# When the first layer's last block pair loads, adds and queues its P4 chunks

## The chip, the cores and the metric

The kernel runs on one core of a Trainium2 chip. The metric is the device time of one execution in microseconds (us), lower is better. PE is TensorE, DVE is VectorE, ACT is ScalarE, POOL is GpSimd; SP is the engine whose queue issues nearly all loads. A line such as L387 is a line of the kernel before; behind the first edit, the changed kernel's lines are 1 to 5 higher.

## The reference

Two layers run one after the other on a stream of 512 tokens with 2048 features. Each layer norms its rows, projects them by one wide matrix, runs two groups of heads on the result, joins the heads, projects them by an output matrix `w_out` of 2048 x 2048, norms again and adds the result to the stream:

```python
    h = rmsnorm(x, g_pre)
    z = h @ w_in
    ...
    y = jnp.concatenate([o_gla, o_att], axis=-1) @ w_out
    return x + rmsnorm(y, g_post)
```

The change lies in the output projection of the first layer, in the second half of its columns.

## The kernel before, in words

**Products.** A projection is cut into blocks of 512 columns, and two blocks make a pair (`fast_gemm`, called at the end of a layer for the pair `W01` and then for `W23`). Each pair is computed with seven products, P1 to P7, instead of eight, on sums and differences of the four quarters of the tokens' matrix and of the weights. A product runs over four chunks of the contraction (c = 0 to 3), and one chunk of one product is a **job**: twelve 128x512 matmuls on PE, all of form L387. Every float32 operand is split into a high and a low part, so each product of numbers costs three matmuls (high x high, high x low, low x high).

**A job's weights.** A `Job` has three steps. `load` issues a 512 KB load of a weight chunk (tile `raw` or `H`) on SP's queue and, for P5, P6, P3 and P7, another 512 KB load of a ready-made sum of tokens (tile `sa`, from the DRAM tensors oS). `high` first forms the weight sum on DVE (L194 adds into H, L196 subtracts from H) and then casts it on ACT to the high part `wh` (L200). `low` takes the difference on DVE to the low part `wl` (L209). In the pair `W23`, P4's chunk is loaded into the ring `raw` at P4's job, and its sum H + raw is formed at P4's job too.

**Order.** The jobs stand in a list that is written by hand; for `W23` it is `PROD_END`: P1 and P2 in turn for the four chunks, then P5 and P6 mixed, then P3, P7 and P4 with four chunks each. That makes 28 jobs; numbered from 0, P6's chunk 1 is job 12 and P4's chunks are jobs 24 to 27. Loads, highs and lows run three to five jobs ahead of PE (`ahead`). A scheduler that works with estimated times then fixes the order of the instructions on each engine. On the chip, each engine and each queue works in that order.

**Ties.** `tc.issue_after(x)` lets the scheduler put an instruction only behind x. In `high` the weight sums of the output projection are put behind `lows[-2]`, the low part of two jobs before.

**What stands around it.** While `W23` runs, the residual's rows are loaded (L457, tiles g, sg and bias, through `residual`), and P7's first chunks are loaded early into the slots a110 to a113. When P3 has ended, rows 0 to 255 of the layer's output are finished: two sums of squares, a reciprocal root on POOL (L429), four row products on DVE (L1383), squares for the next norm on ACT (L442), the norm itself (L497 and L499), transposes on PE (L513), and from them the next layer's operands: an ACT copy with a gain (L524), an ACT cast to the high part and a DVE difference for the low part (both in the helper at L105 and L106), which write the slots a110, a120, a111 and so on. The next layer begins with a plain product (L309) whose first job reads a110, its second a120, its third a111. Rows 256 to 511 follow when P4 has ended, with the same steps.

Of the kernel before, what the change touches and what calls it, by code (L numbers as in the profile page):

```python
# [11 lines left out]
ALU = mybir.AluOpType  # L12
# [11 lines left out]
NB_IN = 14  # L24
# [9 lines left out]
def hybrid_trunk(  # L34
# [13 lines left out]
    nc = tc.nc  # L48
# [16 lines left out]
    def nm(s):  # L65
        serial[0] += 1
        return f"{s}_{serial[0]}"

    def slot(tag, shape, dtype=F32):
        return slots.tile([P] + shape, dtype, tag=tag, name=nm(tag))  # L70

    def rtile(tag, shape=(2, W), dtype=F32, bufs=4):
        return ring.tile([P] + list(shape), dtype, tag=tag, name=nm(tag), bufs=bufs)
# [27 lines left out]
    def flat(t):  # L101
        return t.bitcast(F32).rearrange("p a b -> p (a b)")
# [30 lines left out]
    PROD_OUT = order("10 20 11 21 12 13 50 51 60 61 22 23 52 53 62 63 30 31 32 33 70 71 72 73 40 41 42 43")  # L133
    LEFT = {"P5": "S1", "P6": "S2", "P3": "S4", "P7": "S3", "P4": "A22"}
    SPARE = ("g12", "g13", "g16", "g17")
    lows, last_turn = [], [None]
    last_cast, last_low, last_mm, last_load, last_h = [None], [None], [None], [None], [None]

    class Job:
# [14 lines left out]
        def load(self):  # L154
            k, c, p, b0, b1 = self.kind, self.c, self.pair, self.b0, self.b1
            end = b0 >= NB_IN and k != "std"
            if end:
                c = OC[c]
            top, bottom = (c + 4, c) if end else (c, c + 4)
            mid = end and b0 == W23[0] and self.l < L - 1  # L160
            if k == "std":
                self.raw = self.fetch(rtile("raw", bufs=5), b0, c)
            elif k == "P1":
                p["H", self.c] = self.fetch(rtile("H"), b0, top)
                last_h[0] = last_load[0]
            elif k == "P5":
                p["r", self.c] = self.fetch(rtile("raw", bufs=5), b1, top)
            elif k == "P6":
                p["r", self.c] = self.fetch(rtile("raw", bufs=5), b1, bottom)
            elif k == "P7":  # L170
                p["r", self.c] = p.pop(("t", self.c), None) or self.fetch(rtile("raw", bufs=5), b0, top)
            elif k == "P2" or (k == "P4" and end):
                p["r", self.c] = self.fetch(rtile("raw", bufs=5), b0, bottom)
            sums = (so_d if end else sa_d)[self.l]
            src = sums.get((LEFT.get(k), c))
            if src is not None and b0 != NB_IN and not (k == "P5" and b0 == AV0):
                until(lambda: k == "P4" or (id(sums), LEFT[k], c) in written)
                self.a = rtile("sa", (2, 512), F32R)
                with tc.issue_after(last_h[0]) if mid else nullcontext():
                    last_load[0] = nc.sync.dma_start(flat(self.a), src).ins  # L180
            if b0 == W23[0] and k == ("P6" if mid else "P5"):
                with tc.issue_after(last_h[0]):
                    p["t", self.c] = self.fetch(slot(f"a11{self.c}" if mid else SPARE[self.c], [2, 512]), b0, c + 4)

        def high(self):
            k, c, p = self.kind, self.c, self.pair
            if k == "std":
                src = self.raw
            else:
                h, r = p["H", c], p.get(("r", c))  # L190
                src = h if k in ("P1", "P5", "P6", "P4") else r
                with tc.issue_after(lows[-2]) if self.b0 >= NB_IN else nullcontext():
                    if k in ("P5", "P6") or (k == "P4" and self.b0 >= NB_IN):
                        nc.vector.tensor_tensor(out=h, in0=h, in1=r, op=ALU.add)  # L194
                    elif k == "P7":
                        nc.vector.tensor_tensor(out=r, in0=h, in1=r, op=ALU.subtract)  # L196
            self.src = src
            self.wh = rtile("wh", dtype=F32R)
            for z in self.parts():
                last_cast[0] = nc.scalar.copy(self.wh[:, z, :], src[:, z, :]).ins  # L200
# [70 lines left out]
    def until(cond):  # L271
        while not cond():
            assert tasks or delayed
            pump(1)
# [185 lines left out]
    def load_tokens(half, src):  # L460
        xs = Tokens()
        xs.moves = []
        for j in range(2):
            t = 2 * half + j
            if half == 0:
                row = [slot(tag, [1024]) for tag in XS0[j]]
            elif j == 0:
                row = [slot(tag, [1024]) for tag in XS1]
            else:
                row = [tmp.tile([P, 512], F32, tag=tag, name=nm(tag), bufs=2) for tag in ("sg", "sg", "bias", "bias")]  # L470
            o = 0
            for z in row:
                xs.moves.append((z, src[t * P : (t + 1) * P, o : o + z.shape[-1]]))
                o += z.shape[-1]
            xs.append(row)
        return xs
# [244 lines left out]
    def layer(l):  # L721
# [715 lines left out]
        def residual(k, c):  # L1437
            if last:
                if (k, c) == ("P2", 0):
                    xs[1] = load_tokens(1, x_src)  # L1440
                if k in ("P1", "P2") and xs:
                    xs[1].load(last_h[0], 1)
            elif k in ("P5", "P6") or (k in ("P1", "P2") and c >= 2):
                half = int(k in ("P5", "P6"))
                if half not in xs:
                    xs[half] = load_tokens(half, x_src)
                xs[half].load(last_h[0], 1)

        fast_gemm(l, W23, out_consume(2), rate=3, end=True, lag=2 if last else 0, ops=O, after=residual)
        if not last:  # L1450
            tasks.append(finish(1, xs[1]))
# [57 lines left out]
```

## Time and profile before

| what | value |
|---|---|
| median of 3 runs | 1616.84 us (1616.81 to 1617.41) |
| the profiled execution | 1617.52 us |
| its span, first to last instruction | 1615.5 us |
| PE busy | 1600.5 us, 99% of the span |
| DVE, ACT, POOL busy | 1272.4, 918.5, 131.5 us |
| moved by DMA | 438.17 MB, 271 GB/s on average |
| mean granted clock of PE | 0.998 |

The profile is of one execution. In its timelines a row has the start in us, the time to the end of the last of the grouped instructions, the engine, line, operation, tiles and count, and in brackets the idle time ahead with what ended it. For SP's queue a row tells when loads were issued; the time from there to their landing is given apart. Matmuls overlap, so the interval between two starts is what one costs.

### The profile page before, as it was taken

The page shows a single profiled execution, that of the slowest core. Times are in us where ns is not written, and L with a number is a line of the kernel's source. Part 1 is how long each engine was busy: PE and PEld are TensorE (multiplying, and loading weights), DVE is VectorE, ACT ScalarE, POOL GpSimd, SP SyncE. Part 2 cuts the span into 40 slices and gives each one's busy share as a digit, 9 for nine tenths or more (in the row PEclk, how much of TensorE's full clock was granted, in tenths as well). Part 3 has the DMA queues.
Part 4 walks back from the last instruction along what each step waited for, and adds up shares of the span by engine and source line. Part 5 has one row for each costly group of instructions (what it writes and reads, how often), then busy time and mean ns, then how long its engine had stood idle before and what let it go on. Part 6 is the DMA issues. An engine that isn't in the chain of part 4 may idle for free.

```text
span 1615.5 us, 24476 instructions
## 1 busy us (share of the span) xinstructions
PE 1600.5 (99%) x8938; PEld 1372.8 (85%) x8938; DVE 1272.4 (79%) x1646; ACT 918.5 (57%) x1507; POOL 131.5 (8%) x192
## 2 busy tenths in 40 slices
PE   9999999999999999999999999999999999999997
PEld 7888999998888777888788889999988887788886
DVE  5977778678777878998988677786786878689887
ACT  7544445657455546665696444456675545566654
POOL 0120000010010010100122000000100100101001
PEclk9999999999999999999999999999999999999999
DMA  9797686685867768689779886867858687686986
GB/s 370 263 366 268 240 293 216 226 299 176 286 211 277 268 217 317 223 307 381 265 263 359 330 295 228 305 203 243 309 201 294 208 298 254 222 302 233 342 299 193
DMA packets 133928, 438.17 MB, mean 271 GB/s; under 512 B 14404, under 2 KB 27204, under 8 KB 133776
## 3 DMA queue, kind: packets, MB, share of 16 engines
q1 hardware_dynamic: 117072, 375.99, 66.9%
q0 software_dynamic: 16160, 59.53, 10.0%
q8 instruction: 71, 1.16, 0.3%
q10 hardware_dynamic: 576, 1.08, 0.2%
q14 instruction: 49, 0.40, 0.1%
HBM read 377.02 MB, written 61.62 MB: 272 GB/s over the span
## 4 chain that ended last, share of the span: by engine, by line
PE 94%; DVE 2%; DMA 1%; issue 1%; ACT 1%; POOL 0%; DVEq 0%; SPq 0%; ACTq 0%; POOLq 0%
PE mm L387 53%; PE mm L377 19%; PE mm L309 10%; PE ax L937 2%; PE ax L387 2%; PE ax L1123 1%; PE ax L920 1%; PE ax L744 1%; PE ax L1095 1%; DMA raw<-in_w_dram 1%; PE ax L900 1%; PE ax L899 1%; PE ax L898 1%; DVE wl L209 0%; DMA bias<-in_rel_dram 0%
## 5 line engine op out<-in xcount | busy, mean ns | idle before, releaser
L387 PE MATMUL mm<-wh,sa 128*128 128x512 f32 x1600 | 517.8, 394 | 0.8 <-ACT wh L200 0.5
L200 ACT CAST wh<-H 128x1024 fp32r<-128x1024 f32 x256 | 268.5, 1051 | 217.0 <-PE mm L387 91.6
L209 DVE TENSOR_TENSOR wl<-H,wh 128x1024 fp32r<-128x1024 f32 x256 | 312.3, 1221 | 94.6 <-PE mm L387 37.6
L387 PEld LDWEIGHTS mm<-wh,sa 128*128 128x128 f32 x1600 | 299.5, 188 | 73.0 <-issue 9.4
L200 ACT CAST wh<-raw 128x1024 fp32r<-128x1024 f32 (+1 forms) x233 | 244.1, 1052 | 197.0 <-PE mm L387 89.5
L209 DVE TENSOR_TENSOR wl<-raw,wh 128x1024 fp32r<-128x1024 f32 (+1 forms) x233 | 282.4, 1215 | 61.9 <-PE mm L387 24.5
L387 PE MATMUL mm<-wl,sa 128*128 128x512 f32 x800 | 312.6, 391 | 0.0
L377 PE MATMUL mm<-sa,wh 128*128 128x256 f32 x1280 | 237.4, 285 | 0.0
L387 PE MATMUL mm<-wh,a 128*128 128x512 f32 x640 | 211.5, 394 | 0.0
L377 PEld LDWEIGHTS mm<-sa,wh 128*128 128x128 f32 x1280 | 200.3, 191 | 0.3
L377 PE MATMUL mm<-sa,wl 128*128 128x256 f32 x640 | 180.9, 283 | 0.0
L387 PEld LDWEIGHTS mm<-wl,sa 128*128 128x128 f32 x800 | 150.3, 188 | 30.1 <-DVE wl L209 0.4
L194 DVE TENSOR_TENSOR H<-H,raw 128x1024 f32<-128x1024 f32 x144 | 174.9, 1219 | 1.0
L387 PEld LDWEIGHTS mm<-wh,a 128*128 128x128 f32 x640 | 119.5, 188 | 24.9
L387 PE MATMUL mm<-wl,a 128*128 128x512 f32 x320 | 125.6, 393 | 0.0
L377 PEld LDWEIGHTS mm<-sa,wl 128*128 128x128 f32 x640 | 122.5, 191 | 0.0
L429 POOL TENSOR_TENSOR sm<-sm,mhalf 128x2 f32<-128x2 f32 (+2 forms) x40 | 55.5, 1387 | 764.3 <-DVE sm L947 458.7
L196 DVE TENSOR_TENSOR raw<-H,raw 128x1024 f32<-128x1024 f32 x56 | 68.5, 1223 | 51.1 <-DMA raw<-in_w_dram 50.5
L387 PE MATMUL mm<-wh,g 128*128 128x512 f32 x320 | 101.6, 391 | 0.0
L377 PE MATMUL mm<-a,wh 128*128 128x256 f32 x512 | 95.4, 285 | 0.0
L339 ACT COPY ev<-mm 128x512 f32<-128x512 f32 x104 | 60.7, 584 | 60.2 <-PE mm L387 43.4
L215 DVE TENSOR_TENSOR H<-H,raw 128x1024 f32<-128x1024 f32 x48 | 58.7, 1223 | 35.7 <-DMA raw<-in_w_dram 35.4
(250 smaller groups left out, 2323.8 us busy)
## 6 DMA issues: line engine op xcount, KB each, us to landing
raw<-in_w_dram SPq DMA_DIRECT2D x311, 512.0 KB, 5.2
sa<-S SPq DMA_DIRECT2D x184, 512.0 KB, 4.5
H<-in_w_dram SPq DMA_DIRECT2D x64, 512.0 KB, 5.0
sa<-A SPq DMA_DIRECT2D x48, 512.0 KB, 5.8
S<-g POOLq DMA_DIRECT2D x32, 512.0 KB, 8.7
sa<-oS SPq DMA_DIRECT2D x32, 512.0 KB, 5.3
oS<-g POOLq DMA_DIRECT2D x16, 512.0 KB, 4.4
oS<-sa POOLq DMA_DIRECT2D x16, 512.0 KB, 5.6
```

The costliest lines, as they stand in the source:

```text
L194: nc.vector.tensor_tensor(out=h, in0=h, in1=r, op=ALU.add)
L196: nc.vector.tensor_tensor(out=r, in0=h, in1=r, op=ALU.subtract)
L200: last_cast[0] = nc.scalar.copy(self.wh[:, z, :], src[:, z, :]).ins
L209: last_low[0] = nc.vector.tensor_tensor(out=self.wl[:, z, :], in0=self.src[:, z, :], in1=self.wh[:, z, :].bitcast(F32), op=ALU.subtract).ins
L215: nc.vector.tensor_tensor(out=h, in0=h, in1=self.src, op=ALU.add)
L309: nc.tensor.matmul(pss[o], a(part, kk, o) if callable(a) else a[:, part, t], rhs[:, kk, :], start=(i == 0 and kk == 0 and m == 0), stop=(i ...
L339: nc.scalar.copy(e, src[t])
L377: nc.tensor.matmul(dst, lhs[:, kk, f], a[:, part, tok], start=(fresh and kk == 0 and m == 0 and ft % 2 == 0), stop=(c == 3 and kk == 1 and ...
L387: last_mm[0] = nc.tensor.matmul(out_ps[t], a[:, part, tok], rhs[:, kk, :], start=(fresh and kk == 0 and m == 0), stop=(c == 3 and kk == 1 ...
L429: nc.gpsimd.tensor_tensor(out=out_r, in0=v, in1=mhalf[:, : v.shape[-1]], op=ALU.pow)
L744: nc.tensor.matmul(ps[0:96, half * 256 : (half + 1) * 256], wga[kt // 10][:, kt % 10, :], op[:, i, (kt % 2) * 256 : (kt % 2 + 1) * 256], s ...
L937: nc.tensor.matmul(o, self.pt[i][:, j * P : (j + 1) * P], av[hd // 4, j // 2][:, j % 2, (hd % 4) * P : (hd % 4 + 1) * P], start=(j == 0), ...
```

## The change

Four edits, all for the pair `W23` of the first layer (`mid` in the code):

1. P4's weight chunk is no longer loaded into the ring `raw` at P4's job, but at P3's job of the same chunk, into a slot of its own (`EARLY`: a120, a121, g14, g15; `p["u", c]`).
2. P4's sum H + chunk is formed right behind P7's difference, in P7's `high`, instead of in P4's.
3. The tie of these DVE instructions is looser: behind the low part of four jobs before instead of two.
4. The residual's second half of rows is loaded by the calls behind P3 and P7 instead of those behind P5 and P6.

```diff
+    EARLY = ("a120", "a121", "g14", "g15")
...
-            elif k == "P2" or (k == "P4" and end):
+            elif k == "P2" or (k == "P4" and end and not mid):
                 p["r", self.c] = self.fetch(rtile("raw", bufs=5), b0, bottom)
+            if k == "P3" and mid:
+                p["u", self.c] = self.fetch(slot(EARLY[self.c], [2, 512]), b0, bottom)
...
-                with tc.issue_after(lows[-2]) if self.b0 >= NB_IN else nullcontext():
-                    if k in ("P5", "P6") or (k == "P4" and self.b0 >= NB_IN):
+                with tc.issue_after(lows[-4 if ("u", c) in p else -2]) if self.b0 >= NB_IN else nullcontext():
+                    if k in ("P5", "P6") or (k == "P4" and self.b0 >= NB_IN and ("u", c) not in p):
                         nc.vector.tensor_tensor(out=h, in0=h, in1=r, op=ALU.add)
                     elif k == "P7":
                         nc.vector.tensor_tensor(out=r, in0=h, in1=r, op=ALU.subtract)
+                        if ("u", c) in p:
+                            nc.vector.tensor_tensor(out=h, in0=h, in1=p["u", c], op=ALU.add)
...
-            elif k in ("P5", "P6") or (k in ("P1", "P2") and c >= 2):
-                half = int(k in ("P5", "P6"))
+            elif k in ("P3", "P7") or (k in ("P1", "P2") and c >= 2):
+                half = int(k in ("P3", "P7"))
```

The scheduler places the instructions anew. Three places are shown as the built programs have them.

**SP's queue, while PE works on P1 to P5 of `W23`.** Here raw is a weight chunk in the ring, a11x an early chunk of P7, bias a piece of the residual's rows, g14 to a121 the new slots, and sa_1439 the token sum that job 12 (P6, chunk 1) reads. Before:

```order
L151 DMA a112_1461_7538<-in_w_dram 128x1024
L151 DMA raw_1427_7419<-in_w_dram 128x1024
L151 DMA a113_1466_7562<-in_w_dram 128x1024
L151 DMA raw_1432_7444<-in_w_dram 128x1024
L151 DMA a110_1429_7423<-in_w_dram 128x1024
L151 DMA raw_1438_7470<-in_w_dram 128x1024
L151 DMA raw_1449_7506<-in_w_dram 128x1024
L457 DMA bias_1455_7514<-in_x_dram 128x512
L151 DMA raw_1459_7534<-in_w_dram 128x1024
L151 DMA a111_1440_7474<-in_w_dram 128x1024
L457 DMA bias_1456_7515<-in_x_dram 128x512
L180 DMA sa_1439_7472<-oS203_129 128x1024
```

Now, the last twelve rows up to the same sum; a112, raw_1427, g14_1471 and a113 stand just ahead of them, in this order:

```order
L152 DMA raw_1432_7444<-in_w_dram 128x1024
L152 DMA g15_1477_7637<-in_w_dram 128x1024
L152 DMA a110_1429_7423<-in_w_dram 128x1024
L152 DMA raw_1438_7470<-in_w_dram 128x1024
L152 DMA raw_1449_7506<-in_w_dram 128x1024
L462 DMA bias_1491_7687<-in_x_dram 128x512
L152 DMA a120_1463_7573<-in_w_dram 128x1024
L152 DMA raw_1453_7527<-in_w_dram 128x1024
L152 DMA a111_1440_7474<-in_w_dram 128x1024
L462 DMA bias_1492_7688<-in_x_dram 128x512
L152 DMA a121_1467_7593<-in_w_dram 128x1024
L183 DMA sa_1439_7472<-oS203_129 128x1024
```

All four of P4's chunks (g14, g15, a120, a121) now stand ahead of sa_1439, and nothing that stood ahead of it has gone behind it. The pieces of the residual's second half stand where they stood: the two shown, and the four ahead of a112.

**DVE, at P7's last jobs.** H is the weight sum, wl a low part, and the four products into g16, g17, g12 and g13 are those of the finished rows. Before:

```order
L194 TENSOR_TENSOR H_1393_7277<-H_1393_7277,raw_1514_7811 128x1024
L1383 SCALAR_TENSOR_TENSOR g16_1421_7395<-a122_1326_6929,sm_1503_7754,g16_1421_7395 128x1024
L1383 SCALAR_TENSOR_TENSOR g17_1422_7396<-g0_1441_7476,sm_1503_7754,g17_1422_7396 128x1024
L1383 SCALAR_TENSOR_TENSOR g12_1423_7397<-a123_1329_6935,sm_1503_7754,g12_1423_7397 128x1024
L1383 SCALAR_TENSOR_TENSOR g13_1424_7398<-g1_1444_7482,sm_1503_7754,g13_1424_7398 128x1024
L209 TENSOR_TENSOR wl_1522_7841<-H_1387_7241,wh_1513_7809 128x1024
L194 TENSOR_TENSOR H_1409_7330<-H_1409_7330,raw_1524_7846 128x1024
```

Now:

```order
L1338 TENSOR_TENSOR g1_1444_7482<-t2_1503_7755,t2_1397_7287 128x512
L1377 TENSOR_REDUCE sm_1505_7761<-ssy_1328_6933 128x1
L214 TENSOR_TENSOR wl_1514_7812<-H_1373_7189,wh_1508_7784 128x1024
L1388 SCALAR_TENSOR_TENSOR g16_1421_7395<-a122_1326_6929,sm_1506_7762,g16_1421_7395 128x1024
L1388 SCALAR_TENSOR_TENSOR g17_1422_7396<-g0_1441_7476,sm_1506_7762,g17_1422_7396 128x1024
L1388 SCALAR_TENSOR_TENSOR g12_1423_7397<-a123_1329_6935,sm_1506_7762,g12_1423_7397 128x1024
L1388 SCALAR_TENSOR_TENSOR g13_1424_7398<-g1_1444_7482,sm_1506_7762,g13_1424_7398 128x1024
L214 TENSOR_TENSOR wl_1523_7845<-H_1387_7241,wh_1515_7814 128x1024
```

P4's sums have left this place (they stand among P3's and P7's low parts); the four row products still stand ahead of the low part of P4's chunk 1. On ACT, the copy that frees P7's first accumulator for P4 (L339) has moved behind the squares of g16 and g17 (L442), ahead of which it stood.

**ACT and DVE, at the operands of the next layer's first jobs.** H is here the transposed and scaled tokens, a110, a120 and a111 the operands of the first three jobs, g2, g3 and sm the last steps of rows 256 to 511. ACT before:

```order
L105 CAST a110_1527_7856<-H_1526_7853 128x512
L1329 ACTIVATE t2_1543_7912,ssy_1379_7201<-t2_1542_7910 128x512
L1329 ACTIVATE t2_1568_8039,ssy_1376_7195<-mm_1400_7291 128x512
L105 CAST a120_1529_7866<-H_1526_7853 128x512
L200 CAST wh_1566_8035<-raw_1564_8019 128x1024
```

ACT now:

```order
L105 CAST a110_1527_7857<-H_1526_7854 128x512
L1334 ACTIVATE t2_1568_8039,ssy_1376_7195<-mm_1400_7291 128x512
L205 CAST wh_1566_8035<-raw_1564_8019 128x1024
L1334 ACTIVATE t2_1569_8042,ssy_1379_7201<-mm_1401_7292 128x512
L105 CAST a111_1532_7878<-H_1531_7875 128x512
L529 ACTIVATE H_1547_7930<-ax_1546_7925,gcol_172 128x256 x2
L529 ACTIVATE H_1547_7930<-ax_1549_7936,gcol_172 128x256 x2
L105 CAST a120_1529_7867<-H_1526_7854 128x512
```

DVE now (before, the low part of a120 stood three rows behind that of a110, ahead of g3):

```order
L106 TENSOR_TENSOR a110_1527_7857<-H_1526_7854,a110_1527_7857 128x512
L1338 TENSOR_TENSOR g2_1538_7903<-mm_1400_7291,t2_1396_7285 128x512
L1377 TENSOR_REDUCE sm_1573_8054<-ssy_1376_7195 128x1
L1338 TENSOR_TENSOR g3_1541_7909<-mm_1401_7292,t2_1396_7285 128x512
L1377 TENSOR_REDUCE sm_1573_8054<-ssy_1379_7201 128x1
L106 TENSOR_TENSOR a111_1532_7878<-H_1531_7875,a111_1532_7878 128x512
L214 TENSOR_TENSOR wl_1575_8065<-raw_1564_8019,wh_1566_8035 128x1024
L1388 SCALAR_TENSOR_TENSOR g9_1487_7683<-g8_1377_7197,sm_1574_8055,g9_1487_7683 128x1024
L1388 SCALAR_TENSOR_TENSOR g10_1488_7684<-g2_1538_7903,sm_1574_8055,g10_1488_7684 128x1024
L106 TENSOR_TENSOR a120_1529_7867<-H_1526_7854,a120_1529_7867 128x512
```

The operand a120, which the second job reads, is now made behind a111, which the third job reads: on ACT behind four more copies, on DVE behind two row products that wait for POOL's root of P4's sums.

## The prediction

> **What bounds the kernel now.** I read the page's totals first, then who waited for whom on PE around the change, then the stretches' DMA share, then the timelines of the engines.
>
> ```profile
> span 1615.5 us, 24476 instructions
> PE 1600.5 (99%) x8938; PEld 1372.8 (85%) x8938; DVE 1272.4 (79%) x1646; ACT 918.5 (57%) x1507; POOL 131.5 (8%) x192
> ```
>
> PE is busy for all but 15 us of the span, so a change that takes no matmul away can win only what PE waits in the stretch that it touches. PE's waits from 640 to 860 us:
>
> ```profile
> PE mm L387 <- DVE wl L209: 1.2, 1, 1.2
> PE ax L513 <- ACT g L497: 0.4, 1, 0.4
> PE mm L387 <- ACT wh L200: 0.3, 1, 0.3
> ```
>
> Some 2 us in 220, and one wait makes 1.2 of it:
>
> ```profile
> 790.92 0.40 PE L387 MATMUL mm<-wh,g 128*128 128x512 f32 x1
> ...
> 795.74 0.50 PE L387 MATMUL mm<-wl,g 128*128 128x512 f32 x1 [1.19 <-DVE wl L209]
> ```
>
> P4 begins at 790.9 (job 24), and its second job waits for its low part. This is all that the change can take away; 0.2% of the time, about what a measurement of this kernel can tell from no change, is 3.2 us. So the change cannot be faster by that much, and the question is what it adds. What it moves most is four loads of 512 KB, so the next view is the DMA share by stretches:
>
> ```profile
> core 0: us, PE busy (x) PEld busy (x) DVE busy (x) ACT busy (x) POOL busy (x), PEclk, DMA share, GB/s
> 715.00:760.00 45.00, 45.00 (x199) 36.97 (x198) 37.30 (x39) 23.47 (x34) 0.00 (x0) 1.00 1.02 403
> 760.00:770.00 10.00, 10.00 (x46) 8.29 (x45) 7.13 (x7) 6.49 (x9) 0.00 (x0) 1.00 0.81 282
> ```
>
> From 715 to 760 us the DMA engines are full (share 1.02, 403 GB/s); only behind 760 is there room. PE hides it there, but by how little is seen at job 12 (P6, chunk 1):
>
> ```profile
> L180 SPq DMA_DIRECT2D sa<-oS x1: 327/327/327, 750.0 to 750.0; - x1
> DMA to landing us min/median/max: 7.3/7.3/7.3
> ```
>
> ```profile
> 744.57 2.72 PE ax L387 x12
> 747.29 43.58 PE mm L387 x191
> ```
>
> ```profile
> 758.05 0.62 PE L387 MATMUL mm<-wh,sa 128*128 128x512 f32 x2
> ```
>
> The first fence is the load of job 12's token sum: issued at 750.0, landed 7.3 later, at 757.3. The second, from the chain, shows one job of twelve matmuls at 2.72 us, and that job 8 starts at 747.29. Job 12 is four jobs later, near 758.2; the PE timeline has its first matmul as the second of the pair at 758.05, so at 758.3. The sum lands **1.0 us** before it is needed.
>
> **The change part by part.** The number of instructions stays: 757 loads by SP, as many DVE sums, the same matmuls. What counts is where they stand.
>
> *Edit 1, the loads.* The first of P4's chunks was issued here, and the others after it, behind the full stretch:
>
> ```profile
> 756.99 0.33 SPq L151 DMA_DIRECT2D raw<-in_w_dram  x1
> ```
>  Now all four stand ahead of job 12's sum in SP's queue, in the full stretch. Four times 524,288 bytes at 403 GB/s are **5.2 us**, and the sum lands at 762.5 instead of 757.3. PE waits for it from 758.3: **4.2 us**. That the slots are free in time doesn't help: their last readers are P2's jobs 1, 3, 5 and 7, which end before 747.3, and the queue is bound by the transfers. Behind the waiting matmul stand all later jobs of PE, so nothing else can be done meanwhile. The following sums land 1.3 us apart (512 KB at that rate), PE needs them 2.72 apart: no second wait. P6's last chunk now stands behind one more sum and lands near 765; its addition, cast and low part (1.2, 1.1 and 1.2 us in the rows below) give 768.5, and job 15 comes at 770.7. A wait of PE for a load is not in this stretch of the trace. Its lower bound is 0 (the loads find room); the upper one takes the slowest landing of the stretch, that of the residual's rows:
>
> ```profile
> L457 SPq DMA_DIRECT2D g<-in_x_dram x6: 327/328/430, 721.9 to 732.8; - x6
> DMA to landing us min/median/max: 7.8/9.0/10.7
> ```
>
> Issued 5.2 later and landed after 10.7, the sum would be there at 765.9: 7.6. I take 4.2, from the rate of the stretch itself.
>
> In a sentence apart: the Trainium skill (DMA: Bandwidth & Descriptors, Where 436 GB/s comes from) puts the ceiling at 435 GB/s and the limit of HBM per core at about 358. By these the four loads would take 4.8 or 5.9 us and the wait would be 3.8 or 4.9; the stretch's 403 GB/s lies above the second, so the row decides.
>
> *Edits 2 and 3, the sums and their tie.* Four sums of 1.2 us leave DVE's queue at P7 and P4 and go among the low parts of P3 and P7. What stood at P4:
>
> ```profile
> 786.72 1.21 DVE L209 TENSOR_TENSOR wl<-H,wh 128x1024 fp32r<-128x1024 f32 x1
> 787.85 1.22 DVE L194 TENSOR_TENSOR H<-H,raw 128x1024 f32<-128x1024 f32 x1
> 789.67 1.28 DVE L1383 SCALAR_TENSOR_TENSOR g<-a,sm,g 128x1024 f32<-128x1024 f32 x1 [0.61 <-POOL sm L429]
> ...
> 793.27 1.28 DVE L1383 SCALAR_TENSOR_TENSOR g<-g,sm,g 128x1024 f32<-128x1024 f32 x1
> 794.46 1.22 DVE L209 TENSOR_TENSOR wl<-H,wh 128x1024 fp32r<-128x1024 f32 x1
> ```
>
> The low part of P4's chunk 1 began at 794.5 behind four row products of 1.2; the 1.19 us wait is theirs. Now, with PE 4.2 later, P4 begins at 795.1. The low part of its chunk 0 can start when job 21 is done (three buffers), at 789.7; four products end at 795.6, and chunk 1's low part ends at 796.8. PE's new order takes the first half of chunk 1 ahead of the second half of chunk 0, so it needs that part at 796.7. This wait goes. But the copy of P7's accumulator now stands behind two squares on ACT:
>
> ```profile
> 790.13 0.57 ACT L339 COPY ev<-mm 128x512 f32<-128x512 f32 x1
> 790.99 1.06 ACT L442 ACTIVATE t<-g 128x1024 bf16<-128x1024 f32 x1 [0.28 <-DVE g L1383]
> ```
>
> The second of them waits for the second product (793.2); with the first square (1.06), a cast (0.95), the second square and the copy (0.57) P4's accumulator is free at 795.7, 0.6 late. So 1.2 goes and 0.6 comes: **-0.6 us**, bounds -1.2 and +0.6 (the copy a full row product later).
>
> *Edit 4* moves no load past another in SP's queue; 0.
>
> *What the new placing adds.* The cast and the low part of a120 now stand behind those of a111. Before:
>
> ```profile
> 806.86 0.65 ACT L105 CAST a<-H 128x512 fp32r<-128x512 f32 x1
> ...
> 808.56 0.65 ACT L105 CAST a<-H 128x512 fp32r<-128x512 f32 x1
> 809.07 1.09 ACT L200 CAST wh<-raw 128x1024 fp32r<-128x1024 f32 x1
> 810.02 0.64 ACT L1329 ACTIVATE t<-mm 128x512 bf16<-128x512 f32 x1
> ...
> 812.34 2.36 ACT L524 ACTIVATE H<-ax,gcol 128x256 f32<-128x256 f32 x6
> ```
>
> ```profile
> 809.41 0.68 DVE L106 TENSOR_TENSOR a<-H,a 128x512 fp32r<-128x512 f32 x1
> ...
> 811.88 0.69 DVE L1333 TENSOR_TENSOR g<-mm,t 128x512 f32<-128x512 f32 x1
> 812.48 0.15 DVE L1372 TENSOR_REDUCE sm<-ssy 128x1 f32<-128x5 f32 x1
> ...
> 813.82 2.48 DVE L1383 SCALAR_TENSOR_TENSOR g<-g,sm,g 128x1024 f32<-128x1024 f32 x2
> ```
>
> ```profile
> 807.87 0.47 PE L309 MATMUL mm<-wh,a 128*128 128x512 f32 x1
> ...
> 810.48 0.61 PE L309 MATMUL mm<-wh,a 128*128 128x512 f32 x2
> ```
>
> I count from the start of a110's cast (806.86). Before, a120's low part was done at 3.2, and the second job (from 810.7) first used it 0.45 later, at 4.3. Now ACT does the cast of a110 (0.51, from 808.56 to 809.07), a square (0.6), a cast (0.95), a square (0.6), a111 (0.51) and four copies (0.38 each) before a120, whose high part is ready at 5.2. The second square ends at 2.7; on DVE the product with the gain (0.6) follows, the reduction with POOL's root and the hand-overs (1.34, from 812.48 to 813.82), two row products (2.4) and a120's low part (0.68): ready at **7.7**. PE needs it at 4.3, so it waits **3.4**. ACT has no idle from 800 to 820; its later squares may hold back a110 by up to 0.8 more, as far as I can follow the order. I take **3.8**, bounds 0 (DVE and ACT have the 4.2 us of PE's first wait to get ahead) and 5.
>
> *Sum:* 4.2 - 0.6 + 3.8 = **+7.4 us**, so the profiled execution goes from 1617.52 to 1624.9. That execution lies 0.7 above the median of the three runs; the median goes to **1624.2**. Behind this place PE is full up to the end, so nothing pays it back.
>
> **The rivals.**
>
> *PE's clock falls.* If the 4.2 us without matmuls makes PE run slow afterwards, as it does at the start:
>
> ```profile
> 1.18 4.23 PE L674 MATMUL ax<-t 128*128 128x512 bf16 x10 [1.18 <-DVE t L671]
> ```
>
> Ten matmuls of this shape in 4.2 us are 0.42 each, against 0.227 in a job; 4.2 us at that pace lose 2.0 more: 1626.2. Against it: the span's mean granted clock is 0.998 with the 1.2 us wait at 794 in it; nothing here shows a longer one. In a sentence apart: the Trainium skill (TensorE: Matmul & The Clock Gate, What's actually happening) has PE at half rate after an idle window of some 3.4 us that runs free of the kernel; by that rule a wait of 4.2 would hold a whole window about one time in four, an estimate from the page's figure.
>
> *Only the first wait.* The 4.2 us let ACT and DVE get ahead and a120 is early: 4.2 - 0.6, 1620.4. For it: P4's sums no longer burden DVE there. Against it: the row products need P4's own end.
>
> *The loads find room* (not slower). If the four loads delay the token sum by less than 1.0 us, from which point the first wait decides, PE doesn't wait at job 12, and 3.4 - 0.6 are left: 1619.6, within 0.2%. It would need 4.2 of the four loads' 5.2 us of transfer to be found in a stretch whose share is 1.02 already, which speaks against it. Without the a120 wait too, it would be 1616.2, just the gain that was open.
>
> *The change doesn't do what it says:* edit 4 does so in its queue, at no price either way.
>
> **How the numbers follow.** Forecast 55%; clock 13%; only the first wait 12%; loads find room 10%; both hidden 3%; a wait that I don't see, beyond 1627.5, 6%; faster by over 0.2%, 1%. The first case's own spread (bounds of the two waits) is 1622 to 1626; the range 1620.0 to 1627.5 takes in the clock and the first wait alone and leaves out the rest. Slower by over 0.2%: 55 + 13 + 12 + 6 = 86%; same 13%; faster 1%.
>
> **What would show it.** In the profile after: PE L387 waits some 4 us for DMA sa at P6's chunk 1, near 758; the 1.19 at P4 is gone or at most halved and named ACT; L309 waits 3 to 4 us for a120 from DVE L106 near 815. Wrong if the token sum of job 12 lands before 759, or if L309's second job starts without a wait.

## The result, and the profile after

The changed kernel takes **1628.87 us** (median of 5 runs, 1627.39 to 1630.02) beside 1616.84 (5 runs) of the kernel before, slower by 12.0 us. The medians alone make that 1.0074 times as long; the ratio on record is 1.0065, 95% interval 1.0054 to 1.0077. The forecast was 1624.2, its range 1620.0 to 1627.5: the sign and the two waits are as foretold, the time lies 1.4 us above the range (by the ratio, 1627.4, at its upper edge). The profiled execution took 1630.02, its span is 1628.2.

The page's totals:

```profile
span 1628.2 us, 24480 instructions
PE 1605.8 (99%) x8938; PEld 1375.9 (85%) x8938; DVE 1272.2 (78%) x1646; ACT 919.4 (56%) x1507; POOL 125.9 (8%) x192
```

PE is busy 5.3 us more than before with the same 8938 instructions, and idle 7.4 us more. So waits explain only a part of the 12.7 us between the spans; the rest are the same matmuls, run slower. PE's waits from 640 to 860 us:

```profile
PE mm L392 <- DMA sa<-oS: 5.1, 1, 5.1
PE mm L314 <- DVE a L106: 1.8, 1, 1.8
PE mm L314 <- ACT a L105: 1.6, 1, 1.6
PE mm L392 <- ACT ev L344: 0.5, 1, 0.5
PE mm L392 <- ACT wh L205: 0.3, 1, 0.3
```

The first is job 12, the next two are the next layer's second job with a120, the fourth is P4. The old 1.2 at P4 and 0.4 at the transposes are gone. PE's timeline at job 12 (start, length, engine, line; in brackets the idle time before it and who ended it):

```profile
757.27 0.39 PE L392 MATMUL mm<-wh,sa 128*128 128x512 f32 x1
762.71 0.76 PE L392 MATMUL mm<-wh,sa 128*128 128x512 f32 x1 [5.06 <-DMA sa<-oS]
763.28 0.63 PE L392 MATMUL mm<-wl,sa 128*128 128x512 f32 x1
763.70 1.05 PE L392 MATMUL mm<-wh,sa 128*128 128x512 f32 x2
764.56 0.63 PE L392 MATMUL mm<-wl,sa 128*128 128x512 f32 x1
...
767.12 0.63 PE L392 MATMUL mm<-wl,sa 128*128 128x512 f32 x1
767.54 0.68 PE L392 MATMUL mm<-wh,sa 128*128 128x512 f32 x2
768.06 0.40 PE L392 MATMUL mm<-wl,sa 128*128 128x512 f32 x1
```

After the wait the starts lie 0.43 us apart (three such gaps from 763.28 to 764.56), and 0.23 again from 767.54. The same in windows of the stretch (us of each engine with its count, then granted clock, DMA share, GB/s):

```profile
762.70:767.60 4.90, 4.89 (x12) 3.84 (x13) 1.80 (x2) 1.04 (x1) 0.00 (x0) 0.50 0.81 321
767.60:772.50 4.90, 4.90 (x23) 4.06 (x22) 3.12 (x3) 3.18 (x4) 0.00 (x0) 1.00 0.49 141
822.30:825.70 3.40, 3.40 (x9) 2.64 (x8) 2.69 (x5) 3.40 (x7) 0.00 (x0) 0.50 0.37 142
```

**PE is busy in all of these windows, yet at a granted clock of 0.50 it does half the work**: 12 matmuls where the next window has 23. Below, such a stretch's loss is the sum over all starts more than 0.36 us apart of what each is above 0.227: 2.3 us here, and 1.6 us in the second stretch at 822, behind the waits for a120:

```profile
817.81 0.50 PE L314 MATMUL mm<-wh,a 128*128 128x512 f32 x1 [1.58 <-ACT a L105]
...
820.84 0.73 PE L314 MATMUL mm<-wh,a 128*128 128x512 f32 x2 [1.84 <-DVE a L106]
```

Job 12's load itself, in the DMA view (issued at 753.6, landed 9.0 later, at 762.6):

```profile
L183 SPq DMA_DIRECT2D sa<-oS x1: 327/327/327, 753.6 to 753.6; - x1
DMA to landing us min/median/max: 9.0/9.0/9.0
```

Last, what the prediction did not expect, three small waits from 1000 to 1080 us, in the second layer:

```profile
PE mm L382 <- DVE wl L214: 1.1, 2, 0.6
PE mm L382 <- DMA sa<-S: 0.5, 1, 0.5
```

### The profile page after: what moved, and what is told of

It reads as the page before. It is cut to its first block, busy times and chain, and to the rows that moved or that the text cites. A ratio compares the mean times of both kernels' runs of the same rounds, so it can differ in the third digit from the quotient of the medians.

```text
span 1628.2 us, 24480 instructions
## 1 busy us (share of the span) xinstructions
PE 1605.8 (99%) x8938; PEld 1375.9 (85%) x8938; DVE 1272.2 (78%) x1646; ACT 919.4 (56%) x1507; POOL 125.9 (8%) x192
## 4 chain that ended last, share of the span: by engine, by line
PE 91%; DMA 3%; DVE 3%; issue 1%; ACT 1%; DVEq 0%; POOL 0%; ACTq 0%; SPq 0%; POOLq 0%
PE mm L392 51%; PE mm L382 18%; PE mm L314 11%; PE ax L942 2%; DMA raw<-in_w_dram 2%; PE ax L392 1%; DMA sa<-oS 1%; PE ax L1128 1%; PE ax L925 1%; PE ax L749 1%; PE ax L1100 1%; DVE wl L214 1%; PE ax L905 1%; PE ax L904 1%; PE ax L903 1%
## 5 line engine op out<-in xcount | busy, mean ns | idle before, releaser
L197 DVE TENSOR_TENSOR H<-H,raw 128x1024 f32<-128x1024 f32 x140 | 169.6, 1217 | 2.9 <-DMA raw<-in_w_dram 1.9
L434 POOL TENSOR_TENSOR sm<-sm,mhalf 128x2 f32<-128x2 f32 (+2 forms) x40 | 50.1, 1254 | 757.1 <-DVE sm L952 457.5
L220 DVE TENSOR_TENSOR H<-H,raw 128x1024 f32<-128x1024 f32 x48 | 58.7, 1223 | 39.1 <-DMA raw<-in_w_dram 39.1
```

What stands on the lines that cost most here:

```text
L220: nc.vector.tensor_tensor(out=h, in0=h, in1=self.src, op=ALU.add)
L434: nc.gpsimd.tensor_tensor(out=out_r, in0=v, in1=mhalf[:, : v.shape[-1]], op=ALU.pow)
```

## The experiments

Theory: (1) four loads in the full stretch push job 12's token sum back, PE waits; (2) standing still halves PE's rate for some us; (3) a120's place behind a111 and two row products makes PE wait again, with a second slow stretch. Rivals: the moved sums (edits 2 and 3) cost the time; the slow stretches have another cause; the waits only move on when one is mended. Edit 4 was not run by itself.

### Only the loads moved back

```diff
+                if mid and k == "P6":
+                    last_sum[0] = last_load[0]
-            if k == "P3" and mid:
-                p["u", self.c] = self.fetch(...)
+            if k == "P3" and mid:
+                with tc.issue_after(last_sum[0]):
+                    p["u", self.c] = self.fetch(...)
```

> The changed kernel with one thing put back: P4's four weight chunks are issued behind P6's third token sum instead of ahead of job 12's (P6, chunk 1). The sums stay where the change put them. If the four loads are what made job 12 late: its 5.06 us wait goes (at most 1 us left), the stretch of half-rate matmuls behind it (about 2.3 us) goes with it, the two waits for the next layer's second operand (1.58 and 1.84 us, and 1.6 us of half rate behind them) stay: 1628.9 - 7.4 = about 1621.5 us. Rival, the moved sums and the looser tie cost the time: job 12 waits less but what is gained comes back in P7 or P4, 1626 us or more. Rival, the wait alone costs and the half-rate stretch has another cause: 1623.8 us.

Measured: 1623.72 us (5 runs), 1.0040 of the kernel before (1.0027 to 1.0053). Job 12's wait and the slow stretch behind it are gone, the a120 waits and theirs are not. Of the 7.4 us 5.2 came. The time alone would also fit the rival of 1623.8, in which the slow stretch has another cause; but in this trace that stretch is gone, and a new wait makes up the difference. PE now waits 1.63 us at 769, at P3's first job, and 0.56 at P4. The rows of this kernel at 769 name a copy on ACT, which ends at the same moment; whose wait it is, the spread loads below decide. The moved sums alone don't hold job 12 back.

### Only a120 moved ahead

```diff
...
-            half_lows.append(split(op[:, 0, :], op[:, 1, :], dst))
+            with tc.issue_after(half_casts[1]) if l == 1 and half == 0 and ch == 1 else nullcontext():
+                half_lows.append(split(op[:, 0, :], op[:, 1, :], dst))
+            half_casts.append(casts[-1])
...
-                    with tc.issue_after(last_low[0]) if pair else nullcontext():
+                    with tc.issue_after(half_lows[3]) if pair else nullcontext():
```

> The changed kernel with the loads as they are, and the next layer's second operand (a120) cast on ScalarE ahead of a111 and subtracted on VectorE ahead of pair 1's row products. If the placing behind a111 and two row products is the second cost: the waits of 1.58 and 1.84 us at 817 to 821 us and the 1.6 us of half-rate matmuls behind them go, a wait for a111 of up to 1 us may come instead: 1628.9 - 5.0 = about 1624 us, job 12's wait and its half-rate stretch unchanged. Rival, the waits only mirror that the whole tail is late (another wait takes their place at the next operand): 1627.5 us or more.

Measured: 1624.24 us (5 runs), 1.0046 (1.0034 to 1.0059): 4.6 less than the changed kernel. PE's waits from 640 to 880 us:

```profile
PE mm L394 <- DMA sa<-oS: 4.1, 1, 4.1
PE mm L316 <- ACT a L107: 1.1, 1, 1.1
PE mm L394 <- ACT ev L346: 0.5, 1, 0.5
...
```

Instead of 1.58 and 1.84 with a slow stretch there is one wait of 1.1, without one. Job 12's 4.1 and its slow stretch (2.7 us) stand.

### Both

The two edits above in one kernel.

> The changed kernel with the edits of both runs before it. If the two places are the whole loss, they add: 1628.9 - 7.4 - 5.0 = about 1616.5 us, the time of the kernel before. If a third cost is left (small waits of 0.5 us each at 1046 to 1051 us in the second layer, 2 us in all, seen in the changed kernel's profile alone): about 1618.5 us.

Measured: 1619.88 us (11 runs, 1617.40 to 1622.20), 1.0011 (1.0002 to 1.0021), within 0.2% of the kernel before. Both expectations were too low, since neither had P3's wait in it. The spans differ by 1.7 us (1617.2 and 1615.5). In the changed stretch the waits are 1.48 for P3's first sum, 0.56 at P4, 1.03 for an operand, less the 1.19 and 0.38 that the kernel before has and this one hasn't: 1.5. Outside it, 1.0 us of waits at 956 to 960 us in the second layer and 1.5 us less idle time ahead of 640 us go against each other. No slow stretch, and no waits at 1046 us. So the two places are the whole loss but for about 1.5 us; P3's wait and the operand's came with the mending.

### PE kept busy through the wait

```diff
+            if (l, b0, k, c) == (0, W23[0], "P6", 1):
+                fill, z = ops[1, 1, 0], aux()
+                with tc.issue_after(last_mm[0]):
+                    for i in range(20):
+                        last_mm[0] = nc.tensor.matmul(z, fill[:, 0, 0:P], fill[:, 0, :], ...).ins
...
```

> The changed kernel with 20 idle matmuls (128x512, an operand already in place, into a spare PSUM tile) between job 11 and job 12, so that TensorE works where it stood still for 5.06 us: 20 x 0.227 = 4.5 us. The output is unchanged. If the half-rate stretch comes of TensorE having stood still: job 12's matmuls start 0.227 us apart from the first, about 2.3 us go, 1628.9 - 2.3 = about 1626.5 us. If it comes of something else (the full DMA, power): they start 0.427 us apart all the same, 1629 us.

Measured: 1625.72 us (5 runs), 1.0055 (1.0043 to 1.0068): 3.1 less than the changed kernel, though PE does 20 matmuls more. PE's timeline of this kernel:

```profile
756.90 4.70 PE L416 MATMUL ax<-g 128*128 128x512 f32 x20
761.85 0.47 PE L392 MATMUL mm<-wh,sa 128*128 128x512 f32 x1 [0.25 <-DMA sa<-oS]
762.16 0.39 PE L392 MATMUL mm<-wl,sa 128*128 128x512 f32 x1
762.39 0.62 PE L392 MATMUL mm<-wh,sa 128*128 128x512 f32 x2
...
817.68 1.22 PE L314 MATMUL mm<-wh,a 128*128 128x512 f32 x2 [1.84 <-DVE a L106]
```

```profile
761.90:766.80 4.90, 4.90 (x22) 4.05 (x23) 2.07 (x3) 1.17 (x2) 0.00 (x0) 1.00 1.01 387
```

The sum lands at 761.8, about as late as in the other kernels with the four loads ahead (761.9 to 763.4), the DMA is full (share 1.01), and the matmuls behind run at a granted clock of 1.00. **Standing still is what halves the rate**; the full DMA is not. The slow stretch behind a120, which this edit doesn't touch, is there (2.8 us).

### The kernel before with four idle loads

```diff
...
+            if k == "P3" and mid:
+                nc.sync.dma_start(slot(EARLY[self.c], [2, 512]), w[self.l, b0, bottom].rearrange("p (k n) -> p k n", k=2))
```

> The kernel before the change with one thing added: four loads of 512 KB at P3's jobs, into the buffers that the change uses, which nothing reads; P4 keeps its own loads and sums. The output is unchanged. If the loads' place in the queue is the first cost: job 12 waits 4 to 5 us for its token sum, about 2.4 us of half-rate matmuls follow, and the next layer's operands stay as before: 1617.0 + 7 = about 1624 us. Rival, the moved sums and ties make job 12 late: 1617 us, as before.

Measured: 1625.04 us (5 runs), 1.0046 (1.0033 to 1.0059). PE's timeline:

```profile
763.36 0.77 PE L390 MATMUL mm<-wh,sa 128*128 128x512 f32 x1 [5.33 <-DMA sa<-oS]
802.63 0.50 PE L390 MATMUL mm<-wl,g 128*128 128x512 f32 x1 [1.19 <-DVE wl L212]
808.96 1.53 PE L516 MATMUL ax<-cst,g 128*128 128x128 f32 x12 [0.38 <-ACT g L500]
```

The wait, 5.33, is a little more than the 4 to 5 expected; with 1.7 of slow stretch it makes 7.1 of the 7.5 us. The loads alone do it, with nothing that reads them. P4's old waits of 1.19 and 0.38 are there to the digit, since the sums were not moved: edits 2 and 3 are worth these two less the 0.49 that stands at P4 after, 1.1 us. Small waits in the second layer are here too, 0.9 us in three.

### Two loads ahead, two behind

The first experiment's edit, with the tie for chunks 2 and 3 alone (`if self.c >= 2`).

> The changed kernel with two of the four loads ahead of job 12's token sum and two behind P6's last one. If each load ahead costs its 1.3 us of the full DMA stretch: job 12 waits 4.1 to 5.1 less 2.6, so 1.5 to 2.5 us, and the 1.6 us wait of the run with all four behind goes, since two loads fit there. The waits for a120 stay. Without a half-rate stretch behind the wait: 1623.7 - 1.6 + 2.0 = about 1624 us; if 2 us of standing still are enough to halve the rate: about 1626.4 us.

Measured: 1625.98 us (5 runs), 1.0056 (1.0042 to 1.0070). PE's timeline and the window behind it:

```profile
760.36 0.47 PE L395 MATMUL mm<-wh,sa 128*128 128x512 f32 x1 [2.02 <-DMA sa<-oS]
760.67 0.40 PE L395 MATMUL mm<-wl,sa 128*128 128x512 f32 x1
760.90 1.02 PE L395 MATMUL mm<-wh,sa 128*128 128x512 f32 x2
761.72 0.63 PE L395 MATMUL mm<-wl,sa 128*128 128x512 f32 x1
...
764.27 0.43 PE L395 MATMUL mm<-wl,sa 128*128 128x512 f32 x1
```

```profile
760.50:764.40 3.90, 3.90 (x11) 3.05 (x12) 2.45 (x2) 1.28 (x2) 0.00 (x0) 0.56 1.02 409
```

Half the loads give a wait of 2.02, in the middle of the 1.5 to 2.5 foretold, and the wait at 769 is gone: two loads fit there, four don't. Here 2 us of standing still were enough for a slow stretch, one that began 0.5 us after work had begun again.

### The loads spread, and two tries to mend what came of it

```diff
-                with tc.issue_after(last_sum[0]):
+                with tc.issue_after(last_load[0]):
                     p["u", self.c] = self.fetch(...)
```

This is "both" with each load behind its own job's token sum.

> Both edits of the third run, and each of P4's four loads issued right behind the token sum of its own P3 job, one by one. If the 1.5 us wait at 767 us of that run is P3's first sum standing behind the four loads: it goes, no other takes its place, and the time is that of the third run less 1.5 us, about 1617 us in runs of the same spread, as the kernel before. If the DMA engines have no room there either: a wait of 1 us or more at a later P3 or P7 job, 1618.5 us or more.

Measured: 1621.75 us (8 runs), 1.0025 (1.0015 to 1.0036); slower than "both", and not for the reason of either expectation. No wait is left before P4, so the one at 769 was the sum's. But the earlier operands let the next layer's row squares move ahead of the copies of P7's accumulators on ACT, all four instead of two:

```profile
789.78 1.05 ACT L450 ACTIVATE t<-g 128x1024 bf16<-128x1024 f32 x1
...
791.76 1.05 ACT L450 ACTIVATE t<-g 128x1024 bf16<-128x1024 f32 x1
...
792.82 1.04 ACT L450 ACTIVATE t<-g 128x1024 bf16<-128x1024 f32 x1
...
793.86 0.56 ACT L347 COPY ev<-mm 128x512 f32<-128x512 f32 x1
```

PE waits 3.69 us for that copy, and a slow stretch of 1.6 follows. It is the mechanism of the prediction's 0.6 at P4, with twice the squares. So the squares were tied behind the copies:

```diff
+            while l == 1 and half == 0 and not copied:
+                yield
+            with tc.issue_after(copied[0]) if l == 1 and half == 0 else nullcontext():
                 square_sum(ss[:, j : j + 1], xs[j])
```

> The kernel with the spread loads (the run before the last) with one tie more: the next layer's four row squares of the first token half stand on ScalarE behind the two copies of P7's accumulators, for which P4's first matmul waited 3.7 us there. If that wait, and the half rate of 1.6 us behind it, came of the four squares standing ahead: both go, and what is left is less than the kernel before has (its waits of 1.19 and 0.38 us at P4 and at the transposes do not come back): 1621.8 - 5.2 = about 1616.5 us, or 0.5 to 1 us under the kernel before on the same chip. Rival, the later squares make the transposes or the first operands late: waits of 1 us or more at 800 to 815 us, 1618 us or more.

Measured: 1624.62 us (5 runs), 1.0044 (1.0030 to 1.0057). The rival held, and for more than it said. The copies came in time, the squares too late, behind the last residual squares, and the transposes waited for them:

```profile
792.62 0.50 PE L396 MATMUL mm<-wl,g 128*128 128x512 f32 x1 [1.40 <-DVE wl L217]
805.74 3.86 PE L527 MATMUL ax<-cst,g 128*128 128x128 f32 x16 [4.90 <-ACT g L511]
```

The sixteen transposes took 3.86 us here; in "both" sixteen take 1.91. Half rate again, and the two matmuls behind them have it too. With only the second two squares tied (`and j` in both conditions):

> The kernel of the run before with two of the four squares let ahead of the copies again, as the kernel with both edits had them, and the loads still spread. If each square ahead costs the copies about 1 us and the rows' scaling waits for the fourth square: a wait of 0.5 to 1.5 us at P4, one of 0 to 1.5 us at the transposes, no half rate, a span of 1615.5 to 1617.5 us and a time within 2 us of the kernel before. Rival, VectorE's four row products of pair 0 (1.28 us each) make P4 late whatever ScalarE does: 1.4 us at P4 as in the run before.

Measured: 1619.81 us (10 runs, 1617.24 to 1623.60), 1.0016 (1.0006 to 1.0025), span 1617.6: 1.61 at P4, 1.61 and 0.38 at the transposes, no slow stretch. Each number lies just above what was expected, the time 2.4 us over the kernel before; the wait at P4 is named ACT's copy, not VectorE's products as the rival had it. No version here beats the kernel before; the best two come to within 0.2% of it.

### The changed kernel once more

> The changed kernel once more. If the three small waits at 1046 to 1051 us in the second layer (1.5 us in all) belong to the change, they stand in this profile too; if they are of that one execution, they are gone and the span is shorter by about 2 us. Job 12's wait, its half-rate stretch and the two waits for a120 are there either way.

One run, 1629.08 us, span 1627.3. PE's timeline:

```profile
763.24 0.76 PE L392 MATMUL mm<-wh,sa 128*128 128x512 f32 x1 [3.94 <-DMA sa<-oS]
799.23 0.50 PE L392 MATMUL mm<-wh,g 128*128 128x512 f32 x1 [0.49 <-ACT ev L344]
818.62 0.50 PE L314 MATMUL mm<-wh,a 128*128 128x512 f32 x1 [1.58 <-ACT a L105]
821.65 1.22 PE L314 MATMUL mm<-wh,a 128*128 128x512 f32 x2 [1.84 <-DVE a L106]
```

```profile
763.20:768.90 5.70, 5.67 (x14) 4.49 (x15) 2.98 (x3) 1.63 (x3) 0.00 (x0) 0.51 0.85 337
821.70:826.90 5.20, 5.20 (x13) 4.10 (x14) 4.49 (x7) 4.88 (x9) 0.24 (x2) 0.51 0.50 195
```

The small waits of the second layer are gone. Like ones stand in the second layer of some other kernels' profiles (1.0 us in "both" at 956 to 960, 1.4 with a120 ahead at 967, 0.9 with the four idle loads from 969 to 1047), and others have none; they come and go from profile to profile. The waits at 799 and 818 to 822 repeat to 0.01 us; job 12's changes by 1.1 from one execution to the next (in this one PE came 1.7 us later to it, the sum 0.5), and the slow stretches by 0.4 and 0.9.

## Why the prediction was right in kind and too small

| term | predicted | profile after | once more |
|---|---|---|---|
| job 12 waits for its sum | 4.2 | 5.1 | 3.9 |
| half rate behind it | 0 (a rival: 2.0) | 2.3 | 2.7 |
| P4 and the transposes | -0.6 | -1.1 | -1.1 |
| a120 late | 3.8 | 3.4 | 3.4 |
| half rate behind it | 0 | 1.6 | 2.5 |
| small waits, second layer | 0 | 1.5 | 0 |
| sum | 7.4 | 12.8 | 11.4 |
| span against 1615.5 | | 12.7 | 11.8 |

The three forecast terms add up to 7.4 in the profile after, just as predicted, but that is luck: 5.1, -1.1 and 3.4 are off by +0.9, -0.5 and -0.4. Once more they make 6.2. The table leaves out the waits ahead of 640 us, which differ between executions (of those over 0.3 us, 1.3 in the kernel before, none in the profile after, 1.9 once more), so its sums can agree with the spans to about 1 us only.

**The loads' place: right, shown.** The sum landed at 762.6, computed was 762.5; that it is so close is luck too, since the profiles with four loads ahead lie between 761.8 and 763.4. The four idle loads give the same wait in the kernel before; two loads give 2.0. Of the 0.9 between 4.2 and 5.1, 0.7 is PE's earlier arrival in that execution (757.6, computed was 758.3). The 403 GB/s of the stretch was the right price; the changed kernel's stretch has 406.

**Edits 2 and 3: right, the gain twice the forecast.** The copy stood behind two squares, as foretold, and cost 0.49 where 0.6 was said. Left out was that the 0.38 at the transposes goes too. The four-square version shows the mechanism at 3.7 us.

**a120: right to the digit before the allowance.** The count gave 3.4; the waits are 1.58 and 1.84, in five profiles to 0.01. The added 0.4 for ACT's lateness did not come. Part of this is luck: from a110's cast (812.51) the low part was ready at 8.3 (820.78), not 7.7, with a weight's low part of 1.2 us ahead of the row products; and PE's order uses it at the job's fifth matmul, 0.9 us after its start, not at the third (0.45), as the four matmuls between the two waits show. The two errors, about 0.5 each, cancel. That the placing is the cause is shown by the run that undoes it alone. The rival that DVE and ACT would use PE's first wait to get ahead is out: the a120 waits are the same with job 12's wait (1.58 and 1.84) and without it (1.58 and 1.83, loads moved back).

**The clock: the step that failed.** The prediction had the slow stretch as a rival at 13%, because "nothing here shows a longer one" than a wait of 1.2 us, and it counted one stretch. That was no evidence against it: after its first microseconds the trace of before has no wait long enough to tell. Worse, the rival was priced for job 12 alone, though the forecast held a second standing still of 3.4 us. Both stretches together are 3.9 us here and 5.2 once more; the forecast plus these is 1628.1 to 1629.4, where the result lies. The filler shows the cause for the first stretch; for the second it rests on the same pattern in the granted clock (last section) and on its absence where a120 comes in time. The prediction's one time in four was worked out for a stretch that stands idle as a whole; half of one was enough.

What stays open: what sets off the small waits in the second layer, and why the runs of one kernel lie up to 6 us apart (the kernel before, too: 1616.05 to 1622.23 in 15).

## What to carry to other kernels

A load issued early into a full DMA stretch delayed the first transfer behind it in the same queue by about its own transfer time (here 1.1 to 1.5 us each), whoever reads it; look for a place where the queue has room, count how many loads fit there (here two, not four), and follow the order of the other engines again, since every mended wait lets something else move ahead. Price a wait of TensorE of about 2 us or more, or shorter ones close together, with what comes after it: add some 2 us of half rate (here 1.4 to 2.8) to each one that the forecast holds. When PE's busy time grows with the same instructions, look at the granted clock by windows before looking for another wait.

## What the runs showed of the hardware

How little idle time is enough was not expected. Standing still, and the slow stretch behind it (loss by the starts, as above):

| PE's wait, us | kernel | loss at half rate, us |
|---|---|---|
| 1.03, 1.06, 1.19, 1.40, 1.43, 1.48, 1.61, 1.63 | single waits in seven kernels | 0 |
| 2.02 | two loads ahead | 1.6 |
| 1.58, 1.2 of work, 1.84 | changed kernel, loads moved back, filler, two loads ahead, once more | 1.4 to 2.8 |
| 3.69 | loads spread | 1.6 |
| 3.94, 4.12, 5.06 | once more, a120 ahead, changed kernel | 2.7, 2.7, 2.3 |
| 4.90 | squares tied behind the copies | 2.5 (2.0 of it in the transposes) |
| 5.33 | four idle loads | 1.7 |

No single wait up to 1.63 us did it, each from 2.02 on did, and so did two shorter ones close together. A longer wait didn't cost more afterwards. The Trainium skill (TensorE: Matmul & The Clock Gate, What's actually happening) says that the clock falls after an idle window of about 3.4 us, and that the window runs free of the kernel. The half rate agrees (0.43 against 0.23 us between starts); that the whole window must be idle does not, with one wait of 2.02. The ends of the two slow stretches, 768.9 and 826.9 in the changed kernel once more, are 58.0 us apart, an estimated 17 windows by that page's 3.41 us.

The traces settle how much idle time it takes. In all twelve profiles the times between changes of the granted clock are whole multiples of 3.413 us, and each slow stretch lasts one such window or two (3.41 or 6.83 us, part of it under the wait). Counting PE's idle time in every window, at full clock twelve windows were idle for 51% to 100%, and the half clock followed each of them; all others were idle for 50% or less, and it followed none. These are the two nearest to that limit, each with the window behind it, in the changed kernel once more (PE busy 1.67 of 3.41 us) and in the last experiment with the squares (1.69):

```profile
816.57:819.98 3.41, 1.67 (x7) 0.72 (x5) 3.41 (x6) 3.41 (x10) 1.15 (x3) 1.00 0.17 37
819.98:823.39 3.41, 1.74 (x4) 1.45 (x5) 3.41 (x5) 3.41 (x8) 1.21 (x3) 0.50 0.87 336
```

```profile
801.92:805.33 3.41, 1.69 (x13) 1.46 (x14) 3.12 (x4) 3.41 (x5) 0.93 (x1) 1.00 0.36 83
805.33:808.74 3.41, 3.41 (x20) 2.85 (x19) 1.03 (x2) 3.41 (x10) 0.00 (x0) 1.00 0.76 276
```

The ends of matmuls are modelled, so the limit is about half, not 50% to the digit. In every profile the full clock came back only behind a half-clock window that PE had worked through (idle for 5% at most); four that were idle for 29% to 49% were followed by a second one. From these figures, as an estimate: a wait of 3.4 us or more covers half of some window wherever it falls, one under 1.7 us can't by itself, and between the two its place decides.
